# Attention scores on one core: half of two units' casts on ScalarE, score tiles of three, three and two PSUM banks, one PSUM tile for transposes

## The chip, the core and the metric

The kernel runs on one NeuronCore of a Trainium2 chip. The core has five engines that run their own instruction streams: TensorE (PE in the profile; its weight loads are PEld), VectorE (DVE), ScalarE (ACT), GpSimd (POOL) and SyncE (SP). Here SP only issues DMAs; sixteen DMA engines then move the bytes between HBM (the DRAM) and SBUF (the on-chip memory). TensorE writes its results to PSUM, a small accumulator memory of eight banks, and VectorE or ScalarE copies them from there to SBUF. The metric is the device time of one execution in microseconds (us), lower being better.

## The reference

Queries and keys have the shape (8 batches, 8 heads, 512 positions, 64 features), all float32. The result is one 512 x 512 matrix of scores for each of the 64 heads, also float32:

```python
def reference(q, k):
    scale = 1.0 / np.sqrt(q.shape[-1])
    return (np.einsum('bhqd,bhkd->bhqk', q, k) * scale).astype(np.float32)
```

The inputs are 16.78 MB and the output is 67.11 MB. There is no softmax and no reduction over the scores: every product is written out.

## The kernel before

**Units.** The work is cut into four units (v = 0 to 3) of two batches, that is 16 heads each. A unit is loaded by two DMAs of 2 MB (line 83), keys first and then queries, into one SBUF tile `xf` of the pool `big`. Both DMAs are issued by SP.

**Cast.** `load_and_cast` (line 78) turns each of the two into bfloat16. Each takes two instructions on GpSimd, one for each half s (line 89, tile `xb`, 128 partitions x 2048 elements). The pool for `xb` has six buffers, two for each unit.

**Transposes.** `transpose(v, kb, qb)` (line 106) brings the features to the partition axis. It views pairs of bfloat16 as float32 words and transposes 128 x 128 blocks of words on TensorE, eight of them into one PSUM tile `tp` (lines 117 and 125). `rearrange` (line 95) then copies each `tp` tile to SBUF in four copies of 64 x 512 (line 103): into `kT` for keys and into `qz` for queries. There are four groups for each unit, two of keys and then two of queries. A group is one step of eight transposes and four steps of one copy. The engine of the copies alternates from group to group, VectorE first. `qz` has zeros off its diagonal blocks, so that one matmul serves two heads; the zeros are written once by two VectorE memsets (line 156).

**Scores.** `scores(v, t)` (line 132) computes one output tile of four heads, t = 0 to 3. It does 16 matmuls with 512 columns (line 141), two of them into one PSUM tile `ps` of two banks. After each pair, `evacuate` (line 63) scales the 128 x 1024 results and writes them to the SBUF tile `o`. ScalarE (line 66) and VectorE (line 68) take turns. A complete `o` of 4 MB goes out by one DMA of SP (line 146). There are 16 such tiles, called o0 to o15 below.

**Buffers.** The input tiles `xf` and the output tiles `o` share the pool `big`, which has three buffers used in rotation. Units 0, 1 and 2 take the three buffers. Unit 3 takes the buffer of unit 0 when unit 0's casts are done. Then o0 takes the buffer of unit 1, o1 that of unit 2, o2 that of unit 3, and from o3 on each takes the buffer of the output three places before it. PSUM has two `tp` tiles and two `ps` tiles of two banks each.

**Order.** All compute instructions are pinned, so each engine runs its own in program order. All loads and casts come first in the program, then the transposes of unit 0. After that, the steps of the next unit's transposes are woven into the scores of the current one: `take` (line 148) advances them after a `ps` tile has been evacuated. For unit 0 that is one step after every `ps` tile, and for later units after five of the eight `ps` tiles of an output tile. SP issues the eight load DMAs and then the sixteen output DMAs in that order.

Of the kernel before, what the change touches and what calls it, by code (L numbers as in the profile page):

```python
# [1 line left out]

# [5 lines left out]


@with_exitstack  # L10
def kernel(
    ctx: ExitStack,
    tc: tile.TileContext,
    q: bass.AP,
    k: bass.AP,
    out: bass.AP,
):

    nc = tc.nc
    B, H, S, D = q.shape
    scale = 1.0 / (D ** 0.5)
    P = 128
    UNITS = B // 2
    N = H  # L30
    M = P // (2 * H)
    R = S // M
    J = R // 2
    RO = 8
    U = S // RO
    JP = J // 2
    JJ = J // RO // 2
    W = 8
    IW = W // JJ
    TILES = N // 2  # L40

    f32 = mybir.dt.float32
    bf16 = mybir.dt.bfloat16

    q_r = q.rearrange("(v b) g (m j) d -> v (b g m) (j d)", b=2, j=R)
    k_r = k.rearrange("(v b) g (m j) d -> v (b g m) (j d)", b=2, j=R)
    out_r = out.rearrange("(v b) (t x h) (u i) k -> v (b t) (h u) x (i k)", b=2, x=2, h=2, i=RO)

    consts = ctx.enter_context(tc.tile_pool(name="consts", bufs=1))

    big_pool = ctx.enter_context(tc.tile_pool(name="big", bufs=3))
    bf_pool = ctx.enter_context(tc.tile_pool(name="bf", bufs=6))
    t_pool = ctx.enter_context(tc.tile_pool(name="t", bufs=2))
    tpsum_pool = ctx.enter_context(tc.tile_pool(name="tpsum", bufs=2, space=bass.MemoryType.PSUM))
    psum_pool = ctx.enter_context(tc.tile_pool(name="psum", bufs=2, space=bass.MemoryType.PSUM))


    pinned = tc.keep_in_program_order

    n_evac = 0  # L60
    n_tp = 0

    def evacuate(dst, src):
        nonlocal n_evac
        if n_evac % 2 == 0:
            pinned(nc.scalar.mul(out=dst, in_=src, mul=scale))  # L66
        else:
            pinned(nc.vector.tensor_scalar(out=dst, in0=src, scalar1=scale, scalar2=None,  # L68
                                           op0=mybir.AluOpType.mult))
        n_evac += 1  # L70

    def half(h):
        return slice(h * D, (h + 1) * D)

    def words(ap):
        return ap.bitcast(f32)

    def load_and_cast(v):

        xf = big_pool.tile([P, 2, 2, J * D], f32, name="big")  # L80
        both = []
        for x, src in enumerate((k_r, q_r)):
            nc.sync.dma_start(out=xf[:, x], in_=src[v].rearrange("p (s c) -> p s c", s=2))
        for x in range(2):
            xb = bf_pool.tile([P, JP, 2, D, 2], bf16, name="xb")

            wide = (1, RO)[x]
            for s in range(2):
                pinned(nc.gpsimd.tensor_copy(  # L89
                    out=xb[:, :, s].rearrange("p (g i) d e -> p g e i d", i=wide),  # L90
                    in_=xf[:, x, s].rearrange("p (g e i d) -> p g e i d", e=2, i=wide, d=D)))
            both.append(words(xb.rearrange("p j s d e -> p j (s d e)")))
        return both

    def rearrange(tp, pattern, dst):

        nonlocal n_tp
        copy = (nc.vector.tensor_copy, nc.scalar.copy)[n_tp % 2]
        n_tp += 1
        for s in range(2):  # L100
            src = tp[half(s)].rearrange(pattern, n=N, h=2)
            for h in range(2):
                pinned(copy(out=dst(s, h), in_=src[:, h]))  # L103
                yield

    def transpose(v, kb, qb):


        kT = t_pool.tile([P, N, M, 2, J], bf16, name="kT")
        qz = qzs[v % 2]  # L110
        ts[v] = (kT, qz)
        kw = words(kT)
        qw = words(qz)
        for j0 in range(0, JP, W):
            tp = tpsum_pool.tile([P, W, P], f32, name="tp")
            for j in range(W):
                pinned(nc.tensor.transpose(out=tp[:, j, :], identity=identity, in_=kb[:, j0 + j]))  # L117
            yield
            yield from rearrange(tp, "d j (n h m) -> d h n m j",
                                 lambda s, h: kw[half(h), :, :, s, j0:j0 + W])  # L120
        for i0 in range(0, RO, IW):
            tp = tpsum_pool.tile([P, IW, JJ, P], f32, name="tp")
            for i in range(IW):
                for jj in range(JJ):
                    pinned(nc.tensor.transpose(out=tp[:, i, jj, :], identity=identity,  # L125
                                               in_=qb[:, RO * jj + i0 + i]))
            yield
            yield from rearrange(tp, "d i jj (n h m) -> d h i n m jj",
                                 lambda s, h: qw[half(h), i0:i0 + IW, :, h * U // 2:(h + 1) * U // 2]
                                 .rearrange("d i n (m s jj) -> d s i n m jj", s=2, jj=JJ)[:, s])  # L130

    def scores(v, t):

        kT, qz = ts[v]
        o = big_pool.tile([P, 2, RO, S], f32, name="big")
        for x in range(2):
            n = 2 * t + x
            for i in range(0, RO, 2):
                ps = psum_pool.tile([P, 2, S], f32, name="ps")
                for w in range(2):  # L140
                    pinned(nc.tensor.matmul(out=ps[:, w, :], lhsT=qz[:, i + w, n, :],  # L141
                                            rhs=kT[:, n].rearrange("d m s j -> d (m s j)"),
                                            start=True, stop=True))
                evacuate(o[:, x, i:i + 2, :], ps)
                yield
        nc.sync.dma_start(out=out_r[v, t], in_=o.rearrange("p x i k -> p x (i k)"))  # L146

    def take(steps, count):
        for _ in range(count):
            next(steps, None)  # L150

    identity = consts.tile([P, P], dtype=f32)
    make_identity(nc, identity)
    qzs = [consts.tile([P, RO, N, P], bf16, name=f"qz{n}") for n in range(2)]
    for qz in qzs:
        nc.vector.memset(qz, 0.0)  # L156
    cast = [load_and_cast(v) for v in range(UNITS)]

    ts = {}
    for _ in transpose(0, *cast[0]):  # L160
        pass
    for v in range(UNITS):
        ahead = transpose(v + 1, *cast[v + 1]) if v + 1 < UNITS else iter(())
        for t in range(TILES):
            for n, _ in enumerate(scores(v, t)):

                take(ahead, 1 if v == 0 else int(n in (0, 2, 3, 5, 6)))
        for _ in ahead:
            pass


# [1 line left out]
_INS = ['q', 'k']  # L173
_OUTS = [((8, 8, 512, 512), 'float32')]


# [23 lines left out]
```

## Time and profile before

| quantity | value |
|---|---|
| median of 3 runs | 202.47 us (202.41 to 202.62) |
| the profiled execution's own time | 202.52 us |
| span of its instructions, first to last | 200.7 us |
| HBM traffic | 16.78 MB read, 67.11 MB written, 418 GB/s over the span |
| share of the span used by the main DMA queue's packets, over the 16 DMA engines | 98.3% |
| PE busy | 105.3 us (52%) |
| DVE busy | 106.8 us (53%) |
| ACT busy | 85.0 us (42%) |
| POOL busy | 39.5 us (20%) |
| mean granted TensorE clock | 0.815 of full speed |

The profile is one execution on the chip. Its execution time is 1.8 us above the span, since the span runs only from the first to the last instruction. Busy times of the engines overlap and don't add up to the span. In a list of instructions, the first column is the start in us from the start of the span and the second the length; the text in brackets says how long the engine stood idle before, and what ended that wait. "SPq" is SP's instruction queue, where the DMAs are issued. Arrows point from what is read to what is written, so `big<-ps` is an evacuation. L and a number is the line in the kernel before.

### The profile page before, as it was taken

To read this page: it belongs to the slowest core of one execution; us is meant where nothing else is said; L and a number is where in the kernel's file an instruction comes from. 1 tells how busy PE (TensorE), PEld (TensorE's weight loads), DVE (VectorE), ACT (ScalarE), POOL (GpSimd) and SP (SyncE) were. 2 spreads that over 40 slices of the span, in tenths; PEclk is the share of its full clock that TensorE was granted. 3 is DMA by queue.
4 is the path that set the end of the run, shared out by engine and by line. 5 is a ranking of instruction groups with operands and counts; after the bars stand their busy time and mean duration, and the time that the engine had idled before them with its cause. 6 is when DMAs were issued, how large, how long until landed. Compare 5 with 4: busy or idle time off the path is not lost.

```text
span 200.7 us, 1143 instructions
## 1 busy us (share of the span) xinstructions
PE 105.3 (52%) x384; PEld 45.8 (23%) x384; DVE 106.8 (53%) x98; ACT 85.0 (42%) x97; POOL 39.5 (20%) x22
## 2 busy tenths in 40 slices
PE   0035758566657465478637496748585667510000
PEld 0034535223214131224313122312121111100000
DVE  6705538486475976485749357844444444630000
ACT  2004423864755629253844384366435243620000
POOL 1299999995000000000000000000000000000000
PEclk9999576999699999957999759975858858975555
DMA  6999999999999999999999999999999999999994
GB/s 206 424 444 437 421 421 441 434 395 421 434 424 441 428 431 431 433 426 434 431 428 424 434 441 424 431 431 434 424 431 434 431 424 431 428 437 428 428 428 199
DMA packets 5509, 83.95 MB, mean 418 GB/s; under 512 B 384, under 2 KB 384, under 8 KB 384
## 3 DMA queue, kind: packets, MB, share of 16 engines
q1 hardware_dynamic: 5504, 83.89, 98.3%
q8 instruction: 3, 0.05, 0.1%
q14 instruction: 2, 0.02, 0.0%
HBM read 16.78 MB, written 67.11 MB: 418 GB/s over the span
## 4 chain that ended last, share of the span: by engine, by line
DMA 40%; DVE 10%; PE 8%; ACT 6%; issue 1%; ACTq 0%; SPq 0%; DVEq 0%
DMA out_dram<-big 40%; DVE big L68 9%; PE ps L141 8%; ACT big L66 5%; ACT qz L103 1%; DVE qz L103 1%; ACTq L66 0%; SPq L146 0%; DVEq L68 0%
## 5 line engine op out<-in xcount | busy, mean ns | idle before, releaser
L141 PE MATMUL ps<-kT,qz 128*128 128x512 bf16 x256 | 87.6, 447 | 55.5 <-ACT big L66 41.6
L68 DVE TENSOR_SCALAR big<-ps 128x1024 f32<-128x1024 f32 x64 | 78.4, 1224 | 59.8 <-PE ps L141 37.2
L66 ACT ACTIVATE big<-ps 128x1024 f32<-128x1024 f32 x64 | 65.5, 1023 | 73.0 <-PE ps L141 37.2
L141 PEld LDWEIGHTS <-qz 128*128 128x128 bf16 x256 | 27.2, 106 | 111.0 <-issue 97.5
L89 POOL CAST xb<-big 128x2048 bf16<-128x2048 f32 x16 | 38.8, 2468 | 7.9 <-DMA big<-in_k_dram 7.3
L117 PE MATMUL tp<-identity,xb 128*128 128x128 f32 x64 | 11.6, 346 | 13.4 <-POOL xb L89 13.4
L103 ACT COPY kT<-tp 64x512 f32<-64x512 f32 x16 | 9.2, 577 | 15.3 <-PE tp L117 15.1
L103 DVE COPY kT<-tp 64x512 f32<-64x512 f32 x16 | 11.0, 686 | 6.3 <-PE tp L117 6.0
L117 PEld LDWEIGHTS tp<-identity,xb 128*128 128x128 f32 x64 | 10.5, 184 | 15.2 <-POOL xb L89 13.4
L103 DVE COPY qz<-tp 64x512 f32<-64x512 f32 x16 | 11.0, 687 | 2.7 <-PE tp L125 2.5
L103 ACT COPY qz<-tp 64x512 f32<-64x512 f32 x16 | 9.6, 602 | 2.9 <-PE tp L125 2.7
L125 PE MATMUL tp<-identity,xb 128*128 128x128 f32 x64 | 9.4, 300 | 2.5 <-ACT kT L103 2.5
L125 PEld LDWEIGHTS tp<-identity,xb 128*128 128x128 f32 x64 | 8.5, 156 | 4.3 <-issue 3.3
L156 DVE MEMSET qz<- 128x4096 uint32 x2 | 6.9, 3472 | 2.5 <-PEq L184 1.7
L103 ACT ACT_TABLE_LOAD x1 | 1.3, 1283 | 0.7 <-PEq L184 0.7
masks.py:199 POOL TENSOR_SCALAR_AFFINE_SELECT identity<-identity 128x128 f32<-128x128 f32 x1 | 0.3, 292 | 0.1
masks.py:197 POOL MEMSET identity<- 128x128 f32 x1 | 0.2, 204 | 0.3 <-POOLq L184 0.3
L184 POOL MEMSET const-float32-0.0<- 128x1 f32 x1 | 0.1, 98 | 0.2 <-issue 0.2
L184 POOL MEMSET const-bfloat16-1.0<- 128x1 bf16 x1 | 0.1, 101 | 0.0
L184 POOL MEMSET const-uint8-127<- 128x1 uint8 x1 | 0.1, 101 | 0.0
L184 POOL MEMSET const-float32-1.0<- 128x1 f32 x1 | 0.1, 98 | 0.0
## 6 DMA issues: line engine op xcount, KB each, us to landing
out_dram<-big SPq DMA_DIRECT2D x16, 4096.0 KB, 20.7
big<-in_k_dram SPq DMA_DIRECT2D x4, 2048.0 KB, 18.1
big<-in_q_dram SPq DMA_DIRECT2D x4, 2048.0 KB, 22.7
```

The source lines that it names most:

```text
L66: pinned(nc.scalar.mul(out=dst, in_=src, mul=scale))
L68: pinned(nc.vector.tensor_scalar(out=dst, in0=src, scalar1=scale, scalar2=None, op0=mybir.AluOpType.mult))
L89: pinned(nc.gpsimd.tensor_copy(out=xb[:, :, s].rearrange("p (g i) d e -> p g e i d", i=wide), in_=xf[:, x, s].rearrange("p (g e i d) -> p ...
L103: pinned(copy(out=dst(s, h), in_=src[:, h]))
L117: pinned(nc.tensor.transpose(out=tp[:, j, :], identity=identity, in_=kb[:, j0 + j]))
L125: pinned(nc.tensor.transpose(out=tp[:, i, jj, :], identity=identity, in_=qb[:, RO * jj + i0 + i]))
L141: pinned(nc.tensor.matmul(out=ps[:, w, :], lhsT=qz[:, i + w, n, :], rhs=kT[:, n].rearrange("d m s j -> d (m s j)"), start=True, stop=True))
L156: nc.vector.memset(qz, 0.0)
L184: nc = _bacc.Bacc("TRN2", target_bir_lowering=False, num_devices=1)
```

## The change

The change has four parts.

1. **Cast.** For units 0 and 1, the second half (s = 1) of keys and of queries is cast by ScalarE, with `nc.scalar.copy`. GpSimd keeps the first halves, and all of units 2 and 3. That is four ScalarE instructions of 128 x 2048 elements in place of four on GpSimd.
2. **Order.** `load_and_cast` becomes `load` and `cast`. The program has the loads of units 0 to 2, the cast and the transposes of unit 0, the load of unit 3, the casts of units 1 to 3, and then the scores.
3. **Score tiles.** A `ps` tile has three banks. The eight matmuls of one head pair go into tiles of three, three and two, so an output tile has six evacuations in place of eight: four of 128 x 1536 and two of 128 x 1024. There are still two `ps` tiles.
4. **Transposes.** There is one `tp` tile in place of two. For unit 0, the four copies of a group are shared by ScalarE (h = 0) and VectorE (h = 1). For the other units the groups alternate, now with ScalarE first. The steps are taken after the first five of the six `ps` tiles of an output tile, in unit 0 as well.

PSUM is used in full before and after: 2 x 2 + 2 x 2 banks before, and 1 x 2 + 2 x 3 after. No DMA is added, removed or resized.

```diff
@@ -51,7 +51,7 @@
     big_pool = ctx.enter_context(tc.tile_pool(name="big", bufs=3))
     bf_pool = ctx.enter_context(tc.tile_pool(name="bf", bufs=6))
     t_pool = ctx.enter_context(tc.tile_pool(name="t", bufs=2))
-    tpsum_pool = ctx.enter_context(tc.tile_pool(name="tpsum", bufs=2, space=bass.MemoryType.PSUM))
+    tpsum_pool = ctx.enter_context(tc.tile_pool(name="tpsum", bufs=1, space=bass.MemoryType.PSUM))
     psum_pool = ctx.enter_context(tc.tile_pool(name="psum", bufs=2, space=bass.MemoryType.PSUM))
 
 
@@ -75,18 +75,23 @@
     def words(ap):
         return ap.bitcast(f32)
 
-    def load_and_cast(v):
-
+    def load(v):
         xf = big_pool.tile([P, 2, 2, J * D], f32, name="big")
-        both = []
         for x, src in enumerate((k_r, q_r)):
             nc.sync.dma_start(out=xf[:, x], in_=src[v].rearrange("p (s c) -> p s c", s=2))
+        return xf
+
+    def cast(v, xf):
+
+
+        both = []
         for x in range(2):
             xb = bf_pool.tile([P, JP, 2, D, 2], bf16, name="xb")
 
             wide = (1, RO)[x]
             for s in range(2):
-                pinned(nc.gpsimd.tensor_copy(
+                to_bf16 = nc.scalar.copy if s and v < 2 else nc.gpsimd.tensor_copy
+                pinned(to_bf16(
                     out=xb[:, :, s].rearrange("p (g i) d e -> p g e i d", i=wide),
                     in_=xf[:, x, s].rearrange("p (g e i d) -> p g e i d", e=2, i=wide, d=D)))
             both.append(words(xb.rearrange("p j s d e -> p j (s d e)")))
@@ -94,13 +99,15 @@
 
     def rearrange(tp, pattern, dst):
 
+
         nonlocal n_tp
-        copy = (nc.vector.tensor_copy, nc.scalar.copy)[n_tp % 2]
+        copies = (nc.vector.tensor_copy, nc.scalar.copy)
+        first = len(ts) == 1
         n_tp += 1
         for s in range(2):
             src = tp[half(s)].rearrange(pattern, n=N, h=2)
             for h in range(2):
-                pinned(copy(out=dst(s, h), in_=src[:, h]))
+                pinned(copies[(n_tp + h * first) % 2](out=dst(s, h), in_=src[:, h]))
                 yield
 
     def transpose(v, kb, qb):
@@ -135,13 +142,14 @@
         o = big_pool.tile([P, 2, RO, S], f32, name="big")
         for x in range(2):
             n = 2 * t + x
-            for i in range(0, RO, 2):
-                ps = psum_pool.tile([P, 2, S], f32, name="ps")
-                for w in range(2):
+            for i in range(0, RO, 3):
+                wide = min(3, RO - i)
+                ps = psum_pool.tile([P, 3, S], f32, name="ps")
+                for w in range(wide):
                     pinned(nc.tensor.matmul(out=ps[:, w, :], lhsT=qz[:, i + w, n, :],
                                             rhs=kT[:, n].rearrange("d m s j -> d (m s j)"),
                                             start=True, stop=True))
-                evacuate(o[:, x, i:i + 2, :], ps)
+                evacuate(o[:, x, i:i + wide, :], ps[:, 0:wide])
                 yield
         nc.sync.dma_start(out=out_r[v, t], in_=o.rearrange("p x i k -> p x (i k)"))
 
@@ -154,17 +162,19 @@
     qzs = [consts.tile([P, RO, N, P], bf16, name=f"qz{n}") for n in range(2)]
     for qz in qzs:
         nc.vector.memset(qz, 0.0)
-    cast = [load_and_cast(v) for v in range(UNITS)]
+    xfs = [load(v) for v in range(3)]
 
     ts = {}
-    for _ in transpose(0, *cast[0]):
+    for _ in transpose(0, *cast(0, xfs[0])):
         pass
+    xfs.append(load(3))
+    casts = [None] + [cast(v, xfs[v]) for v in range(1, UNITS)]
     for v in range(UNITS):
-        ahead = transpose(v + 1, *cast[v + 1]) if v + 1 < UNITS else iter(())
+        ahead = transpose(v + 1, *casts[v + 1]) if v + 1 < UNITS else iter(())
         for t in range(TILES):
             for n, _ in enumerate(scores(v, t)):
 
-                take(ahead, 1 if v == 0 else int(n in (0, 2, 3, 5, 6)))
+                take(ahead, int(n < 5))
         for _ in ahead:
             pass
 
```

## Prediction, made before the changed kernel ran

> **What bounds the kernel now.** I read the page's slices first, because the busy shares (PE 52%, DVE 53%, ACT 42%) name no full engine.
>
> ```profile
> span 200.7 us, 1143 instructions
> ...
> DMA  6999999999999999999999999999999999999994
> GB/s 206 424 444 437 421 421 441 434 395 421 434 424 441 428 431 431 433 426 434 431 428 424 434 441 424 431 431 434 424 431 434 431 424 431 428 437 428 428 428 199
> ...
> q1 hardware_dynamic: 5504, 83.89, 98.3%
> ```
>
> The DMA engines are busy in every slice but the first and last, whatever the compute engines do. So I cut the span where the rate changes. Columns: stretch and length in us, busy us and instructions of PE, PEld, DVE, ACT and POOL, granted clock, DMA share, GB/s.
>
> ```profile
> 1.00:4.00 3.00, 0.00 (x0) 0.00 (x0) 2.34 (x1) 1.02 (x1) 0.29 (x1) 1.00 0.71 202
> 4.00:40.00 36.00, 17.48 (x75) 11.93 (x76) 18.90 (x19) 11.93 (x17) 31.02 (x13) 0.86 1.01 431
> 40.00:42.00 2.00, 1.52 (x9) 0.71 (x8) 1.03 (x1) 1.30 (x3) 2.00 (x2) 1.00 0.93 328
> 42.00:197.00 155.00, 86.28 (x302) 33.19 (x301) 84.52 (x79) 70.51 (x78) 5.78 (x3) 0.81 1.01 431
> 197.00:199.00 2.00, 0.00 (x0) 0.00 (x0) 0.00 (x0) 0.00 (x0) 0.00 (x0) 0.50 0.52 221
> 199.00:200.70 1.70, 0.00 (x0) 0.00 (x0) 0.00 (x0) 0.00 (x0) 0.00 (x0) 0.50 0.00 0
> ```
>
> Loads alone run at 431 GB/s (to 40 us), and stores alone too (from 42 us). All 83.89 MB at 431 take 194.6 us. The other 6.1 us of the span are 1 us before the first byte, 1.6 us of slow start (3 us at 202), 0.5 us in 40 to 42 where the queue passes from loads to stores, 1.0 us at 221 before the end, 1.7 us without bytes, and 0.3 us of rounding. Only the 0.5 us lies where the change could touch it. The kernel is bound by bytes unless the queue runs dry.
>
> So I ask how early each output is issued. The timeline has start, length, engine, line:
>
> ```profile
> 18.33 0.33 SPq L83 DMA_DIRECT2D big<-in_k_dram  x1
> 18.70 0.43 SPq L83 DMA_DIRECT2D big<-in_q_dram  x1
> ...
> 36.81 11.07 SPq L146 DMA_DIRECT2D out_dram<-big  x2
> ...
> 56.55 35.79 SPq L146 DMA_DIRECT2D out_dram<-big  x5
> ...
> 63.63 1.02 ACT L66 ACTIVATE big<-ps 128x1024 f32<-128x1024 f32 x1 [1.14 <-DMA out_dram<-big]
> ...
> 73.32 1.02 ACT L66 ACTIVATE big<-ps 128x1024 f32<-128x1024 f32 x1 [3.14 <-DMA out_dram<-big]
> ```
>
> The last load, issued at 18.70, takes 24.3 us to land (the answer on the query tensor), so loads end at 43.0. o0 is issued at 36.81, o1 at 36.81 + 11.07 - 0.39 = 47.49, o2 at 56.55. The two waits at 63.6 and 73.3 end when o1 and o2 have landed, 9.7 us apart, which is 4.19 MB at 431 GB/s. Counting back, o0 lands at about 53.8 and its bytes follow the loads without a gap. With 1 us from issue to first bytes (the first load: 0.74, bytes in 1 to 2), the latest harmless issues are about 42.0 for o0, 52.5 for o1 and 62 for o2. The margins are 5.2, 5.0 and 5.5 us. In the steady state the chain of waits shows an output issued at 64.24 landing 18.66 us later, twice 9.7: one whole output always waits in the queue, about 9 us of margin.
>
> **What the Trainium skill says.** "DMA: Bandwidth & Descriptors", Specifications, gives a ceiling of 435 GB/s for the sixteen engines; the trace has 431, 99% of it. Its section on queues says that each DMA engine consumes a ring's descriptors in order; the trace agrees, since stores issued at 36.81 wait behind loads landing at 43.0. "ScalarE: Activation LUTs", What ACT_TABLE_LOAD costs, prices an activation with immediates at 186 ns + 0.833 ns per element; for 1024 elements that is 1039 ns against 1023 in the trace. "PSUM — Partial Sum Buffer", Specifications, has eight banks; 2 + 3 + 3 fill them.
>
> **The change part by part.** Durations are from these groups, mean ns before the last bar:
>
> ```profile
> L68 DVE TENSOR_SCALAR big<-ps 128x1024 f32<-128x1024 f32 x64 | 78.4, 1224 | 59.8 <-PE ps L141 37.2
> L66 ACT ACTIVATE big<-ps 128x1024 f32<-128x1024 f32 x64 | 65.5, 1023 | 73.0 <-PE ps L141 37.2
> ...
> L89 POOL CAST xb<-big 128x2048 bf16<-128x2048 f32 x16 | 38.8, 2468 | 7.9 <-DMA big<-in_k_dram 7.3
> ```
>
> *Prices that the trace lacks.* A ScalarE cast of 2048 elements has no row. By the skill's price it is an estimated 1.9 us; the writes are to every second bfloat16, so I bound it at 1.7 and at 5 us (twice the GpSimd cast) and take 1.9. An evacuation of 1536 elements: ScalarE 1023 + 512 x 0.833 = 1.45 us; VectorE grows by (1224 - 686)/512 = 1.05 ns per element from the 64x512 copy, so 1224 + 538 = 1.76 us.
>
> *Unit 0.* Keys land at 8.55 (GpSimd starts at 8.58), queries at 13.4. Both key halves are ready at 11.05 rather than 13.44. The first eight transposes (16 took 3.68) end at 12.9. Now the costs: ScalarE's two copies of that group stand behind its query cast, 13.4 to 15.3, and finish at 16.5. With one `tp`, group 2 may start only then: transposes to 18.4, two copies on each engine to 19.8. Query groups (16 transposes took 2.57, so 1.3 each): 21.1, copies 22.5, 23.8, copies 25.2. Before, the last copy ended at 24.7. The 2.4 us won by the cast are lost to the single `tp`: net +0.5 us.
>
> *o0.* Behind those copies on ScalarE now stand unit 1's two casts, 25.2 to 27.1 and to 29.0, and its first evacuation behind them: 29.0 rather than 28.13. On PE, unit 1's first transposes stand between the first and second score tile and wait for the key cast: 27.1 to 29.0. The second tile's matmuls follow to 30.0, VectorE 30.0 to 31.8. Then on ScalarE a copy, an evacuation of 1.02, a copy: 33.1; VectorE's second tile of three (matmuls to 33.0) to 34.8; ScalarE's last to about 35.5; two banks' matmuls from 34.8 to 35.6; VectorE to 36.8. o0 is issued near 36.9, against 36.81.
>
> *Unit 3's load* needs unit 0's casts, over at 13.4 + 2.47 = 15.9 rather than 18.3. Behind it on SP are only the outputs, and ahead of it the DMA queue holds loads until 33. Worth 0.
>
> *o1* needs unit 2's casts, all on GpSimd. Its queries land at 3.44 + 29.6 = 33.0 and two casts follow: 38.0, as before (37.96). VectorE then has 2 x 1.76 + 1.22 + 4 copies of 0.69 = 7.5 us: issue near 46.5. *o2* waits for unit 3's casts: 43.0 + 2 x 2.47 = 47.95, as before (48.07), issue near 56.5. Both stay ahead of 52.5 and 62.
>
> *Later outputs.* In each output tile VectorE has 4.74 us of evacuation rather than 4.90, ScalarE 3.92 rather than 4.09. With two `ps` tiles, each engine waits for its own refill: 0.68 us for two matmuls at full clock, 1.10 at half (idle times in the timeline), so 0.98 and 1.63 for three. VectorE: 4.74 + 2 x 0.98 + 0.68 = 7.4 against 7.6; at half clock 9.1 against 9.3. The copies and the single `tp` fall into those waits, as now. A fill stays near the present 9 us, under the 9.7 of its store, and the 9 us of margin cover single slow fills.
>
> *Around the span* nothing changes; 32 evacuations fewer are compute that already hides under the DMAs.
>
> Sum: 0 us of DMA bytes, 0 us of gaps. The profiled 202.52 stays, and that is 0.05 above the median, so I predict 202.5. The cover of all of it is the 5 us by which o0 and o1 are early; without it, each us that o0 is late would be a us of time.
>
> **The rivals.** *The queue runs dry between loads and stores (slower).* Three ScalarE casts stand in a row before the first evacuation, so o0 comes at 36.9 + 3 (c - 1.9) for a cast of c us. It passes 42.0 at c = 3.6; at 5 us o0 is issued at 46.2 and the time is 206.7. If each ScalarE half also waited for GpSimd's half of the same tile, o0 would come near 39.5 and the point would be c = 2.8. For it: three casts and one `tp` lie on the path to o0. Against it: the skill's price, and VectorE's and ScalarE's interleaved writes to `kT` overlap in the trace (15.45 to 18.24 and 17.15 to 19.5), so parts of one tile are not serialised. *Evacuation becomes the bound (slower).* Fills above 9.7 us on average would eat the 9 us of margin; with 14 fills from there, they must average over 10.4 us. At 11 us the time is about 202.5 + 14 x 1.3 - 9 = 212. The sum above says 7.4 to 9.1, so this needs copies that do not hide. *The handover improves (faster).* If the 0.5 us of 40 to 42 went away, 202.0. Nothing says that it hangs on compute: o0 is issued 3 us before it in both kernels. *The casts gain nothing* because everything on the way to o0 is gated elsewhere is already in the forecast, with the same 202.5.
>
> **How the numbers follow.** What a measurement of this kernel can tell from no change is about 0.2%, 0.4 us. Forecast of no change: 0.80, of which the time within 202.2 to 202.8. Dry queue: 0.10, from just visible to 206.7. Evacuation bound: 0.03. Better handover: 0.07. So faster 0.07, same 0.80, slower 0.13. The range reaches to the full handover gain and to a small gap: 202.0 to 203.2.
>
> **What would show it.** DMA share of 1.0 and some 431 GB/s from 4 to 197 us; o0 issued between 36 and 40 us and o1 before 52; a ScalarE cast near 1.9 us; evacuations of 1.45 and 1.76 us; `tp` transposes of unit 0 from 11 us on, with waits on copies between groups; all outputs from the fourth on with landings 9.7 us apart. A slice under 390 GB/s other than the first, the ninth and the last, or o0 issued after 42 us, would make the prediction wrong on the slow side; a ninth slice at 430, on the fast side.

## The result and the profile after

The changed kernel takes 208.11 us (median of 4 runs, 207.60 to 208.46) against 202.48 us before. The ratio is 1.0275, with a 95% interval of 1.025 to 1.03. The forecast was no change, 202.5 us. The profiled execution took 207.88 us, with a span of 206.1 us; the difference is 1.8 us, as before. So the loss of 5.4 us lies inside the span.

The page of the changed kernel, slices and main queue:

```profile
span 206.1 us, 1113 instructions
...
DMA  6999999919999999999999999999999999999994
GB/s 213 436 426 436 429 429 426 432 80 407 455 404 436 429 410 448 413 412 448 405 432 432 410 448 417 432 426 423 436 426 407 442 420 445 413 417 445 420 436 191
...
q1 hardware_dynamic: 5504, 83.89, 96.3%
```

The ninth slice, 395 GB/s before, is at 80. The later slices swing between 404 and 455, where they lay between 421 and 441. The same kernel cut by stretches (columns as in the prediction):

```profile
4.00:41.00 37.00, 13.30 (x50) 9.32 (x52) 11.88 (x11) 17.45 (x16) 22.52 (x10) 1.00 1.01 430
41.00:42.00 1.00, 0.96 (x4) 0.32 (x4) 0.65 (x1) 0.97 (x2) 1.00 (x1) 1.00 0.58 246
42.00:46.00 4.00, 2.77 (x17) 1.67 (x17) 2.33 (x2) 3.48 (x3) 3.97 (x3) 1.00 0.00 0
46.00:48.00 2.00, 0.89 (x4) 0.37 (x4) 1.99 (x2) 1.03 (x1) 1.77 (x1) 1.00 1.21 508
48.00:202.00 154.00, 81.91 (x306) 35.16 (x310) 85.09 (x68) 67.80 (x63) 0.00 (x0) 0.81 1.00 426
```

The loads fill 0.57 us of the second row (246 of 431 GB/s), so I put their end at 41.57 us. Then nothing moves until 46.0. That is an idle stretch of 4.4 us; the hand-over before had lost 0.5 us in the same place, so this costs 3.9 us. And the stores, which ran at 431 GB/s, now run at 426: 67.11 MB take 157.5 us instead of 155.7, another 1.8 us. The sum of 5.7 us compares with 5.4 in the spans. The first two us of stores, at 508 GB/s, are 0.4 us ahead of 431, which would make up the difference.

Why the stores start so late shows in the timeline of unit 0's first key group. DVE and ACT each do two of its four copies, and the bracket names what ended each wait:

```profile
15.74 0.57 ACT L110 COPY kT<-tp 64x512 f32<-64x512 f32 x1
...
16.34 0.68 DVE L110 COPY kT<-tp 64x512 f32<-64x512 f32 x1 [6.94 <-ACT kT L110]
17.06 0.58 ACT L110 COPY kT<-tp 64x512 f32<-64x512 f32 x1 [0.75 <-DVE kT L110]
17.68 0.69 DVE L110 COPY kT<-tp 64x512 f32<-64x512 f32 x1 [0.65 <-ACT kT L110]
```

The two engines take turns: each copy waits for the other engine's copy. VectorE had been idle since 9.4 (6.94 us) and could have read the transposes from 13.1 on, but it waited until ScalarE, after its query cast, had made the first copy. The same pattern repeats in all four groups, and the last copy of unit 0 ends at 32.70 us (24.7 before). Behind it stand the two casts of unit 1, then the first evacuation, then the first output DMA:

```profile
32.72 2.46 ACT L94 CAST xb<-big 128x2048 bf16<-128x2048 f32 x1
...
35.05 2.50 ACT L94 CAST xb<-big 128x2048 bf16<-128x2048 f32 x1
37.63 1.45 ACT L66 ACTIVATE big<-ps 128x1536 f32<-128x1536 f32 x1
...
45.09 0.40 SPq L154 DMA_DIRECT2D out_dram<-big  x1
```

o0 is issued at 45.09 us, 8.3 us later than before, and its bytes start 0.9 us after that.

### The profile page after: what moved, and what is told of

Its sections match the earlier page's. It is cut to its first block, busy times and chain, and to the rows that moved or that the text cites. A ratio compares the mean times of both kernels' runs of the same rounds, so it can differ in the third digit from the quotient of the medians.

```text
span 206.1 us, 1113 instructions
## 1 busy us (share of the span) xinstructions
PE 99.8 (48%) x377; PEld 46.8 (23%) x384; DVE 104.3 (51%) x82; ACT 92.0 (45%) x85; POOL 30.0 (15%) x18
## 3 DMA queue, kind: packets, MB, share of 16 engines
HBM read 16.78 MB, written 67.11 MB: 407 GB/s over the span
## 4 chain that ended last, share of the span: by engine, by line
DMA 31%; DVE 16%; PE 10%; ACT 5%; issue 2%; ACTq 0%; DVEq 0%; SPq 0%
DMA out_dram<-big 31%; DVE big L68 12%; PE ps L149 8%; ACT big L66 5%; DVE kT L110 3%; PE tp L124 1%; DVE qz L110 1%; PE tp L132 0%; ACT kT L110 0%; ACTq L66 0%; DVEq L68 0%; SPq L154 0%
## 5 line engine op out<-in xcount | busy, mean ns | idle before, releaser
L68 DVE TENSOR_SCALAR big<-ps 128x1536 f32<-128x1536 f32 (+1 forms) x48 | 75.8, 1580 | 59.0 <-PE ps L149 37.7
L149 PE MATMUL ps<-kT,qz 128*128 128x512 bf16 x249 | 78.8, 437 | 54.2 <-ACT big L66 32.3
L66 ACT ACTIVATE big<-ps 128x1536 f32<-128x1536 f32 (+1 forms) x48 | 62.8, 1309 | 67.4 <-DMA out_dram<-big 37.5
L94 POOL CAST xb<-big 128x2048 bf16<-128x2048 f32 x12 | 29.3, 2467 | 17.2 <-DMA big<-in_k_dram 12.2
L124 PE MATMUL tp<-identity,xb 128*128 128x128 f32 x64 | 11.9, 349 | 21.2 <-POOL xb L94 11.1
L124 PEld LDWEIGHTS tp<-identity,xb 128*128 128x128 f32 x64 | 10.0, 182 | 24.2 <-issue 12.4
L132 PE MATMUL tp<-identity,xb 128*128 128x128 f32 x64 | 11.8, 346 | 6.7 <-DVE qz L110 2.8
L94 ACT CAST xb<-big 128x2048 bf16<-128x2048 f32 x4 | 9.7, 2466 | 9.0 <-DMA big<-in_k_dram 6.5
L132 PEld LDWEIGHTS tp<-identity,xb 128*128 128x128 f32 x64 | 9.7, 179 | 9.8 <-issue 9.0
```

Source lines behind the costliest of these rows:

```text
L94: pinned(to_bf16(out=xb[:, :, s].rearrange("p (g i) d e -> p g e i d", i=wide), in_=xf[:, x, s].rearrange("p (g e i d) -> p g e i d", e=2, ...
```

## The experiments

The theory was: the change costs time only because the first outputs come after the loads' last byte (41.57 us, so an issue after about 40.7), and what makes them late is a chain of engines' turns, one `tp` tile and ScalarE's casts. The main rival was that the three-bank score tiles slow the stores. Every ratio below is against the kernel before.

### All casts on GpSimd again

```diff
-                to_bf16 = nc.scalar.copy if s and v < 2 else nc.gpsimd.tensor_copy
+                to_bf16 = nc.scalar.copy if s and v < 0 else nc.gpsimd.tensor_copy
```

> The changed kernel with all casts back on GpSimd. Theory (the first output is late, and each us past about 40.7 us of issue costs one us): unit 0's keys are ready at 13.44 rather than 11.1, but no copy waits for a ScalarE cast; four groups of about 4.7 us (transposes 1.94, four copies in turn 2.65) end near 32.4, as late as before in the changed kernel (32.7). ScalarE has no unit 1 casts of 4.9 us ahead of its first evacuation, so o0 starts near 32.5 instead of 37.6, is issued near 40.0, and there is no gap: 202.5 to 203. Rival (the larger score tiles slow the stores by themselves, 426 instead of 431 GB/s): 204 to 205.

Measured: 204.95 us (203.44 to 205.13), ratio 1.0104 (1.0072 to 1.0137). Unit 0's last copies end near 32.5 and o0's evacuation starts at 32.52, both as expected. But o0 is issued at 42.24, since its fill (from its first evacuation to its issue) takes 9.7 us instead of 7.5. Unit 1's first transposes (1.94 us, 32.59 to 34.53), which had run beside ScalarE's casts, now stand inside the fill, ahead of the second score tile. So a gap remains (no bytes from 42 to 43), and the time is above what the theory had. Taking the casts away wins 3.2 us, the larger part of the loss.

### Only unit 0's casts shared

```diff
+                to_bf16 = nc.scalar.copy if s and v < 1 else nc.gpsimd.tensor_copy
```

> The changed kernel with only unit 0's casts shared, unit 1's on GpSimd alone. Theory: unit 0's last copy stays at 32.7, the two ScalarE casts of 4.9 us behind it are gone, o0 starts at 32.8 and is issued near 40.2, just ahead of the end of the loads: 202.5 to 203. Rival (store rate): 204 to 205, with no idle stretch of the DMA engines but 426 GB/s.

Measured: 204.57 us (203.77 to 205.31), ratio 1.0101 (1.0069 to 1.0133). o0 starts at 32.92 and is issued at 41.21, 1 us later than expected. There is no whole us without bytes, yet the stores run at 426 GB/s (48 to 197 us) and the time is 2.1 us up: the numbers of the rival. In windows of a tenth of a us, though, the loads stop at 41.6 and the stores start at 42.1, and only one tenth between has bytes: the queue was empty for about half a us. Which of the two is behind the lower rate was left to the runs with two-bank tiles below.

### Engines share a group by PSUM bank

```diff
-                pinned(copies[(n_tp + h * first) % 2](out=dst(s, h), in_=src[:, h]))
+        for c in range(2 if first else 1):
...
+                    pinned(copies[(n_tp + c) % 2](out=to, in_=frm))
```

Here c counts the two banks of `tp`, each half of its columns.

> The changed kernel, but in unit 0 the two engines share a group by PSUM bank (ScalarE one bank, VectorE the other, four copies of 64x256 each) rather than by head. If the turns are a matter of the bank, both engines run at once, a group's copies take about 1.7 us rather than 2.65, four groups save 4 us, o0 is issued near 41 and the time is near 203.5. If the turns hold for the whole PSUM tile whatever part is read, eight smaller copies in turn take about 3.2 us, o0 comes 2 us later than in the changed kernel (near 47) and the time is near 210.

Measured: 210.76 us (210.39 to 211.45), ratio 1.0411 (1.0392 to 1.0430), o0 issued at 48.09, 1 us later than the second branch has it. DVE of this kernel, then ACT:

```profile
17.04 1.73 DVE L116 COPY kT<-tp 64x256 f32<-64x256 f32 x4 [7.63 <-ACT kT L116]
```

```profile
15.52 1.48 ACT L116 COPY kT<-tp 64x256 f32<-64x256 f32 x4
22.71 1.50 ACT L116 COPY kT<-tp 64x256 f32<-64x256 f32 x4 [5.71 <-DVE kT L116]
```

VectorE's four copies from one bank wait for ScalarE's four from the other. The turns hold for the PSUM tile as a whole. The Trainium skill, "PSUM — Partial Sum Buffer", section Terms, says that two engines on one bank and quadrant (32 partitions) at once are an error, reads against reads included. That is a reason for a program to order such reads, and in the changed kernel both engines read the same banks and partitions. Here the order is coarser than that rule: the program waits even where the two engines use different banks.

### No sharing of unit 0's groups

```diff
-        first = len(ts) == 1
+        first = 0
```

> The changed kernel without sharing of unit 0's groups: one engine copies a whole group, ScalarE first, then VectorE. Theory (sharing gains nothing, as the engines take turns): a group's copies still take 2.3 to 2.8 us and unit 0's last copy ends near 32.4, but on VectorE; ScalarE is free at 27.6 and does unit 1's casts from 27.6 to 32.5 beside the last group. o0 starts near 32.6, is issued near 40.1: 202.5 to 203. If sharing did gain time, this kernel would be slower than the changed one, above 208.

Measured: 205.01 us (203.47 to 206.05), ratio 1.0117 (1.0074 to 1.0161). This is 3.1 us faster than the changed kernel. A group takes 2.3 or 2.4 us on ScalarE alone and 2.8 on VectorE alone, against 2.6 to 2.7 shared, so sharing made the copies no shorter. What is won is that ScalarE is free earlier: it does unit 1's casts from 27.48 on, beside VectorE's last group (29.52 to 32.3), and o0's evacuation starts at 32.38, as expected. The fill again takes longer, and o0 is issued at 43.30 instead of 40.1, so the time is 2 us above the expectation.

### The casts and the order alone

The PSUM tiles, the copies and the steps are as before; only parts 1 and 2 of the change are in.

```diff
-    tpsum_pool = ctx.enter_context(tc.tile_pool(name="tpsum", bufs=1, space=bass.MemoryType.PSUM))
+    tpsum_pool = ctx.enter_context(tc.tile_pool(name="tpsum", bufs=2, space=bass.MemoryType.PSUM))
-            for i in range(0, RO, 3):
+            for i in range(0, RO, 2):
...
```

> Parts 1 and 2 of the change alone: ScalarE's casts and the new order, with two transposing tiles, two-bank score tiles and the steps as before. Theory: with two transposing tiles unit 0's last ScalarE copy ends near 21.4, unit 1's casts fill 21.4 to 25.7 (its queries land at 23.3), o0 starts near 25.8 and is issued near 33.5, earlier than before (36.8), and nothing comes of it: 202.2 to 202.7. A theory that the ScalarE casts themselves are the loss would have 205 or more.

Measured: 202.50 us against 202.50, ratio 0.9999 (0.9990 to 1.0007). The casts do no harm by themselves. My times on the way were too early: o0's evacuation starts at 28.92 and it is issued at 38.15, not 33.5. That is still ahead of the loads' end, so nothing shows.

### The kernel before, with the first output made late

ScalarE gets extra copies of 128 x 2048 (float32 zeros to bfloat16) after unit 0's transposes: two, two and a half, three, and four. They write to a spare tile. In the runs with two and four, every second one writes to every second element. The edit of the run with four:

```diff
     for _ in transpose(0, *cast[0]):
         pass
...
+    for n in range(4):
+        to = spare[:, :, 0] if n % 2 else spare.rearrange("p a b -> p (a b)")[:, 0:2048]
+        pinned(nc.scalar.copy(out=to, in_=zeros))
```

> The kernel before with two added ScalarE copies of 2048 elements (float32 to bfloat16, the first written to adjacent elements, the second to every second one) between unit 0's transposes and the first evacuation. They write to a tile that nobody reads. At 1.9 to 2.5 us each, o0 starts at 29 to 29.7 and is issued at 38 to 38.5, ahead of 40.7: no change, 202.3 to 202.7. If the margin did not exist, 203.5 or more. If the write to every second element is what makes the cast 2.46 us, the first copy takes 1.9 and the second 2.46.

Measured: 202.64 us (202.39 to 202.96), ratio 1.0003 (0.9995 to 1.0012), o0 at 38.31. No change, as expected.

> The kernel before with two and a half added ScalarE copies (2048, 2048 and 1024 elements) between unit 0's transposes and the first evacuation; they write to a tile that nobody reads. Two moved the issue of the first output to 38.3 and cost nothing, four to 44.1 and cost 3.2 us. Here it should be near 39.6. If time grows smoothly from 39.7 on, as the profiled spans so far suggest (200.7 up to 38.3, then 202.2 at 41.2, 203.3 at 42.2, 204.3 at 43.3, 205.2 at 44.1, 206.1 at 45.1, 209.1 at 48.1), no change: 202.4 to 202.8.

Measured: 202.65 us (202.50 to 202.89), ratio 1.0002 (0.9993 to 1.0011), o0 at 37.88, since the copies to adjacent elements are short. No change.

> The same with three added copies: first output near 41.1, barely past the 40.7 at which the load bytes end less 0.9 us. If only the idle stretch counts, it loses 0.4 us less the hand-over: 202.5 to 202.9. If a late first output also lowers the rate of all later stores (426 rather than 431 GB/s), a step of 1 to 1.9 us stands at the threshold: 203.5 to 204.5, with two-bank score tiles.

Measured: 202.88 us (202.56 to 203.83), ratio 1.0026 (1.0015 to 1.0037), o0 at 39.66 rather than 41.1. So this run lies at the threshold, not past it, and doesn't test a step as it was meant to. The loss is small and no us is without bytes. Of the 20 executions 12 lie between 202.56 and 202.94 us and 6 between 203.53 and 203.83, while kernels that are safely ahead spread over 0.7 us at most. The profile is one of the 12, so what happened in the 6 isn't recorded.

> The kernel before with four such ScalarE copies. o0 starts near 33.5 to 34.5 and is issued at 42.5 to 43.2, 1.8 to 2.5 us past 40.7. If lateness alone costs time, a gap of that length opens between loads and stores, less the 0.5 us of the hand-over: 203.8 to 204.5. If a run with a gap also stores at 426 rather than 431 GB/s, 1.8 us more: 205.6 to 206.3, with score tiles of two banks.

Measured: 205.68 us (204.95 to 207.00), ratio 1.0164 (1.0125 to 1.0203); the profiled execution took 207.00, o0 at 44.07, later than the 42.5 to 43.2 expected. Windows of that kernel:

```profile
4.00:40.00 36.00, 14.78 (x53) 10.16 (x54) 14.83 (x16) 16.57 (x15) 30.94 (x13) 0.88 1.01 430
42.00:44.00 2.00, 1.32 (x6) 0.41 (x5) 1.22 (x1) 1.65 (x3) 1.99 (x2) 1.00 0.00 0
48.00:197.00 149.00, 86.05 (x304) 34.41 (x302) 85.03 (x79) 70.59 (x78) 0.00 (x0) 0.82 1.01 427
```

This kernel has no part of the change: two-bank score tiles, two `tp` tiles, all casts on GpSimd. A late o0 alone gives it both signs, the idle stretch and the lower store rate. This refutes the rival as the cause of these two signs.

The same runs price the cast. The four copies, by the tile they write:

```profile
L167 ACT CAST spare<-qz x4: 1898/2182/2467, 25.9 to 32.3; 128x2048 bf16<-128x2048 f32 x4
```

1898 ns to adjacent elements and 2467 ns to every second one. The kernel's own casts have the second form (2466 ns).

### One-bank transposing tiles, two of them

The changed kernel with two `tp` tiles of one bank: groups of four transposes, whole groups to one engine, two steps after each score tile. ScalarE's casts and the three-bank score tiles stay.

```diff
-    W = 8
+    W = 4
-        first = len(ts) == 1
+        first = 0
-                take(ahead, int(n < 5))
+                take(ahead, 2)
...
```

> The changed kernel with two transposing tiles of one bank each (groups of four transposes and four copies of 64x256, engines by turns of whole groups, two steps after each score tile), the three-bank score tiles and the ScalarE casts kept. Theory: transposes of one group run beside the copies of the other, unit 0's last ScalarE copy ends near 25, unit 1's casts near 30, o0 is issued near 38: 202.3 to 202.8. Rival (three-bank tiles slow the stores): 204 to 205.

Measured: 202.53 us (202.40 to 202.83), ratio 1.0003 (0.9994 to 1.0012), o0 at 38.17. Stores run at 430 GB/s with three-bank tiles. Copies from two different `tp` tiles run at the same time, into the same `kT` (ACT, then DVE):

```profile
18.29 1.50 ACT L110 COPY kT<-tp 64x256 f32<-64x256 f32 x4 [1.21 <-PE tp L124]
```

```profile
19.14 1.73 DVE L110 COPY kT<-tp 64x256 f32<-64x256 f32 x4 [4.44 <-PE tp L124]
```

ScalarE is busy until 19.79 and VectorE starts at 19.14. These copies write the same pieces of `kT` and `qz` as the copies by bank above, which took turns. So the shared destination isn't what makes the engines take turns; the shared PSUM tile is. Nothing beats the kernel before here: this version and the casts alone equal it, since their store queue never runs dry either.

### The queue runs dry in mid-kernel

The kernel before, with seven ScalarE copies ahead of the second output tile of unit 1.

```diff
...
         for t in range(TILES):
+            if (v, t) == (1, 1):
+                for n in range(7):
+                    pinned(nc.scalar.copy(out=spare.rearrange("p a b -> p (a b)")[:, 0:2048], in_=zeros))
```

> The kernel before with seven added ScalarE copies of 2048 elements (15.3 us) ahead of the second output tile of unit 1, so that the store queue runs dry in mid-kernel and not at the hand-over from loads. The sixth output should be issued near 95 us, 4 us after its store could have begun: a gap near 95. If an empty queue by itself lowers the rate of what follows, stores run at 431 GB/s up to the gap and 426 after it, and the time is 206.5 to 207.5. If the lower rate belongs to a late hand-over from loads to stores, 431 on both sides and 205.5 to 206.5. The eleven outputs after the gap are 46.1 MB, 107 us at 431, so the two differ by 1.3 us; the windows tell them apart.

Measured: 204.91 us (204.31 to 205.21), ratio 1.0109 (1.0089 to 1.0130). The seven copies took 13.46 us rather than 15.3, so the sixth output came at 91.54, not 95, and the time is below both forecasts. The windows decide:

```profile
48.00:84.00 36.00, 16.37 (x65) 6.94 (x66) 18.58 (x17) 28.13 (x24) 0.08 (x1) 0.83 1.01 431
...
91.00:92.00 1.00, 1.00 (x7) 1.00 (x6) 0.48 (x1) 0.90 (x1) 0.00 (x0) 0.50 0.11 41
...
104.00:197.00 93.00, 49.21 (x164) 18.15 (x165) 47.84 (x43) 40.74 (x45) 0.00 (x0) 0.77 1.01 427
```

Stores run at 431 before the empty moment and at 427 after it, within one execution. The lower rate follows an empty queue in mid-kernel as well as at the hand-over.

### The first output in two halves

The changed kernel, with o0 sent as two DMAs of 2 MB, each as soon as it is complete.

```diff
+                if (v, t, i) == (0, 0, 6):
+                    nc.sync.dma_start(out=out_r[v, t][:, x], in_=o[:, x].rearrange("p i k -> p (i k)"))
                 yield
...
```

> The changed kernel, with the first output sent in two DMAs of 2 MB, each as soon as its four evacuated head rows (one of the tile's two head pairs) are complete. All compute stays as late as in the changed kernel. The first half should be issued near 40.9 and the second near 45.1, before the first half's 4.9 us of bytes are over. If the empty queue is all that the change costs, the time falls back to 202.5 to 203.5. If slower evacuation or transposes in later units cost time too, it stays above 205.

Measured: 207.62 us (206.64 to 207.86), ratio 1.0237 (1.0210 to 1.0264). The time lies where the second forecast has it, but not for its reason. The halves went out at 41.08 and 45.75, and the loads handed over without an idle us. The gap came one tile later:

```profile
41.08 5.02 SPq L154 DMA_DIRECT2D out_dram<-big  x2
54.67 7.66 SPq L157 DMA_DIRECT2D out_dram<-big  x2
...
51.00:52.00 1.00, 0.27 (x2) 0.15 (x2) 0.97 (x2) 0.68 (x1) 0.00 (x0) 1.00 0.63 262
52.00:55.00 3.00, 2.38 (x15) 1.35 (x14) 2.56 (x3) 1.85 (x2) 0.00 (x0) 1.00 0.02 5
```

The first two lines are from the timeline, the last two from the windows. o0's bytes are over at 51.6, and o1, issued at 54.67, starts them again at 55.5. In the changed kernel outputs are issued at 45.09, 53.62, 61.94 and 70.47, some 8.5 us apart. To keep the DMAs busy from 41.57 on they would be due at about 40.7, 50.4, 60.1 and 69.8, 9.7 apart. Each of the first four is late, by 4.4, 3.2, 1.8 and 0.7 us. Sending o0 earlier only moves most of the gap to o1; what must come earlier is the whole chain.

### Issue time against span

| kernel | o0 issued, us | span, us | store rate at the end of the run, GB/s |
|---|---|---|---|
| before | 36.81 | 200.7 | 430 |
| casts and order alone | 38.15 | 200.7 | 430 |
| one-bank `tp` tiles | 38.17 | 200.7 | 430 |
| before, two and a half extra copies | 37.88 | 201.1 | 430 |
| before, two extra copies | 38.31 | 200.6 | 430 |
| before, three extra copies | 39.66 | 201.1 | 429 |
| only unit 0's casts | 41.21 | 202.2 | 427 |
| all casts on GpSimd | 42.24 | 203.3 | 426 |
| no sharing | 43.30 | 204.3 | 426 |
| before, four extra copies | 44.07 | 205.2 | 426 |
| changed | 45.09 | 206.1 | 426 |
| shared by bank | 48.09 | 209.1 | 426 |

These are the profiled executions of all kernels whose queue could run dry only at the hand-over. The rate is that of the window from 55 to 197 us. From 41.21 to 48.09, 6.88 us of issue, the span grows by 6.9 us: one for one. Up to 38.3 it stays within 0.5 us, and the medians within 0.2. From 41.21 on, 202.2 + (issue - 41.21) gives the span of every kernel to within 0.2 us, whatever else they differ in. Followed back to an issue at 40.7, this line gives 201.7, 1.0 us above the kernel before: a part of the loss does not grow with the lateness, as a lower rate to the end would have it. In executions without a profile the issue time isn't known; the medians lie up to 1.3 us from the executions shown here.

## Why the prediction was wrong

**What bounds the kernel: right.** DMA bytes set the time, and a us of empty queue is a us lost. The rival "the queue runs dry between loads and stores" was the outcome; it had 0.10, and its sign, o0 after 42 us, came true. But it came by another way than the rival's, which rests on the price of a cast: with the 2.47 us that a cast took, its own formula, 36.9 + 3 (c - 1.9), gives 38.6 us for o0, which would have been harmless.

**The step that failed: unit 0's copies.** The prediction has "two copies on each engine to 19.8" for a group, that is two engines at work at once. They took turns. The four groups' copies took 2.63, 2.64, 2.65 and 2.71 us, 10.6 in all, where the prediction has 5.4 (1.2 and three times 1.4): 5.2 of the 7.5 us by which the last copy was late (32.7 against 25.2). The evidence used against serialisation was the overlap of writes to `kT`. In the trace of before (the third line is the last copy of unit 0):

```profile
15.45 2.79 DVE L103 COPY kT<-tp 64x512 f32<-64x512 f32 x4 [6.04 <-PE tp L117]
17.15 2.35 ACT L103 COPY kT<-tp 64x512 f32<-64x512 f32 x4 [15.13 <-PE tp L117]
...
22.21 2.50 ACT L103 COPY qz<-tp 64x512 f32<-64x512 f32 x4 [2.70 <-PE tp L125]
```

The overlap is real, but the two engines read two different `tp` tiles there. No two engines read one PSUM tile at once in the trace of before, so the trace could not answer, and the cost should have been bounded from both sides. With both ends, o0 would have been bounded at 36.9 and 42.1, and the second is past the threshold.

**Query transposes: mis-sized.** Eight took 1.94 us, not 1.3. I halved a row of sixteen back to back. With one `tp`, TensorE stands idle between groups, and each of unit 0's groups of eight then took 1.94 us; eight amid score matmuls took 1.04:

```profile
28.01 1.94 PE L132 MATMUL tp<-identity,xb 128*128 128x128 f32 x8 [2.84 <-DVE qz L110]
...
44.23 1.04 PE L124 MATMUL tp<-identity,xb 128*128 128x128 f32 x8
```

The Trainium skill, "TensorE: Matmul & The Clock Gate", Part 1, has the engine at half its clock after an idle window. The trace agrees in size: before, at a granted clock of 0.50, eight took 1.92 us (at 24.40). But in the changed kernel the granted clock reads 1.00 in both places, so it isn't shown that the clock is the reason. With the waits around them this term, second key group included, is 1.8 us.

**ScalarE's cast: mis-sized.** 2.47 us instead of 1.9. It moved the first copy by 0.4 us and unit 1's two casts by 1.0 (4.82 against 3.8). The price in the Trainium skill, "ScalarE: Activation LUTs", What ACT_TABLE_LOAD costs, fits a write to adjacent elements (1898 ns against the estimated 1892), not a write to every second bfloat16. The range given, 1.7 to 5, held it.

These four terms, 5.2 + 1.8 + 0.4 + 1.0, less 0.4 for a fill of 7.5 instead of 7.9, give 8.0 of the 8.2 us between the forecast of 36.9 and 45.09.

**The margin: too wide.** I took 42.0 as the latest harmless issue, from loads that land at 43.0. A landing comes after the last byte: in the changed kernel the last load lands at 16.31 + 26.4 = 42.7, and its bytes end at 41.57. The latest issue is about 40.7, and the run at 39.66 already shows a first trace of loss.

**o1 and o2: right on their own gates, wrong in the chain.** Unit 2's casts do free o1's buffer near 38, but o1's fill can't begin before o0's ends. The run with o0 in two halves shows what that means: o1 is late too. (The prediction's own terms, 38.0 and 7.5 us, give 45.5 for o1; its 46.5 has 1 us without a term. Neither is near the 53.62 measured.)

**What held.** The groups of the changed kernel, shapes kept apart, mean ns before the last bar:

```profile
L68 DVE TENSOR_SCALAR big<-ps 128x1536 f32<-128x1536 f32 x32 | 56.2, 1758 | 50.1 <-PE ps L149 29.7 <-DMA out_dram<-big 16.2 <-issue 2.0
L66 ACT ACTIVATE big<-ps 128x1536 f32<-128x1536 f32 x32 | 46.4, 1451 | 56.7 <-DMA out_dram<-big 37.5 <-PE ps L149 18.3 <-issue 0.4
...
L94 ACT CAST xb<-big 128x2048 bf16<-128x2048 f32 x4 | 9.7, 2466 | 9.0 <-DMA big<-in_k_dram 6.5 <-DMA big<-in_q_dram 2.4
```

The evacuations are the 1.76 and 1.45 us of the forecast, and both engines still wait for output DMAs (16.2 and 37.5 us), so evacuation never became the bound. No loss in later outputs shows from three-bank tiles or one `tp`: the kernel before with four extra copies has neither and stores at the same 426 GB/s. There is no change of bytes, nor around the span. That a dry queue also costs 1.2% of rate afterwards was not foreseen; it is 1.8 us of the loss.

## What to carry to other kernels

Where a saturated DMA queue bounds a kernel, the number to work out is how early each transfer is issued against the last byte of the one before it, and for the whole first chain of transfers, not the first alone. Two engines that share the reading of one PSUM tile may be made to take turns by the program; overlap seen between different tiles is no evidence for one tile. Giving whole tiles to engines by turns, with a second small tile and smaller groups, did what sharing did not (202.53 against 208.11 us).

## What the runs showed that was not expected

After the queue has been empty once, stores run at 426 to 427 GB/s to the end, against 430 to 431 otherwise (429 in the run at the threshold), with two-bank and three-bank tiles alike and after a gap in mid-kernel as well. In the changed kernel, outputs whose landing ends a wait are 9.7 us apart, except two gaps of 10.41 and 10.56 us (waits that end at 107.58 and 166.64). Before, the gaps in the same two places of the sequence were 9.94 and 9.99 us (at 102.66 and 161.16). So 1.0 of the 1.8 us of lost rate sits in these two places. Why they exist, and why an empty queue makes them longer, stays open. The bytes also come in bursts after an empty queue. In the 97 tenths of a us from 100.0 on, the GB/s have a standard deviation of 428 in the changed kernel and of 201 before, and 28 tenths against none carry no bytes. But bursts alone don't explain the rate: with one-bank `tp` tiles, whose queue never runs dry, the deviation from 180.0 on is 336 at a rate of 430.

Runs of kernels near or past the threshold also spread more (4 runs of all casts on GpSimd lie between 203.44 and 205.13 us, 31 of the kernel before between 202.37 and 203.07). What decides between the ends of that spread stays open too.
